# Loading the left half of B tile by tile instead of in pairs of tiles, in a matmul with RMS norm

## The chip, the cores and the metric

One core of a Trainium2 chip runs the whole program. The metric is the time of one execution on the device in microseconds (us). Runs of a kernel are compared with runs of the kernel before that were made on the same chip in the same rounds.

## The reference

```python
m, k, n = 2048, 2048, 2048          # a: m x k, b: k x n, float32
x = np.matmul(a, b)
rms = np.sqrt(np.mean(x ** 2, axis=-1, keepdims=True) + eps)
return (gamma * x / rms).astype(np.float32)
```

## The kernel before

Sixteen contraction tiles of 128 rows of B are handled as eight pairs. B is cut into a left and a right half of 1024 columns. In the head of the program the first four row blocks of A are multiplied with B while B is still arriving; later row blocks find all of B in the on-chip memory and use seven instead of eight products (Strassen's scheme) for each 2 x 2 of blocks. So only the head, about the first 57 us, can wait for B.

Left half: for each pair PE (TensorE) runs 7 matmuls with the first tile, 8 transposes for A of the next pair, 7 matmuls with the second tile, and 2 matmuls for the one block left over. (Pair 7, the last, has no next pair, and takes its matmuls block by block, so that its second matmul already needs the second tile.) The loads come from GpSimd's software queue and cast float32 to bfloat16 on the way: for each pair one load of A (four row blocks, 0.5 MB read), then one load of B (both tiles, 1 MB read).

```python
def load_b(j, kp):                       # j: half of B, kp: pair of contraction tiles
    nc.gpsimd.dma_start(
        out=raw[j][kp],                  # [128, 2, 1024] bf16
        in_=b[kp * W2:(kp + 1) * W2, j * HALF:(j + 1) * HALF].rearrange(
            "(t p) n -> p t n", p=P))

def load_head(kp):
    nc.gpsimd.dma_start(out=ah(kp), in_=a[0:HB * P, kp * W2:(kp + 1) * W2].rearrange(...))
    load_b(0, kp)
# ... pairs 1 to 3 are issued at the start; pair 0 comes over other queues ...
for kp in range(KP):                     # the left half
    if kp + 4 < KP:
        load_head(kp + 4)
    else:
        load_later(1)                    # right half of B, then A
    before = [lambda: transpose_head(kp + 1)] if kp + 1 < KP else []
    # ...
    stream(groups1, kp, before, ...)     # 7 matmuls, `before`, 7 matmuls
    # ...
    stream_in_parts(last1, kp)           # 2 matmuls
    # ... sums of B's quarters on DVE (VectorE) ...
# ...
for kp in range(KP):                     # the right half: 8 + 3 matmuls for a pair
    load_later(1)
    b_sums(1, kp)
    stream_right(kp)
    # ...
```

## Time and profile before

| | before |
|---|---|
| median of the first 3 runs | 222.82 us (222.45 to 223.1) |
| PE busy | 210.0 of 221.2 us |
| a left pair (A and B) lands every | 3.83 us; PE needs 3.89 us for it |
| a right pair of B lands every | 2.49 us; PE needs 2.38 us for it |

The page of the profile gives the span, the busy time of each engine, and the chain of work that ended last. PE is nearly always busy, and the loads of B are the only other large part of the chain. The profiled execution took 222.97 us, more than the median of this kernel's runs.

```profile
span 221.2 us, 3022 instructions
...
PE 210.0 (95%) x1035; PEld 97.7 (44%) x1035; DVE 167.4 (76%) x330; ACT 128.1 (58%) x263; POOL 29.4 (13%) x59
...
PE 83%; DMA 8%; POOL 3%; DVE 2%; issue 1%; ACT 1%; DVEq 0%; ACTq 0%; POOLq 0%
```

The timeline of PE in the head follows. The columns are start and duration in us, engine, source line, operation, output and inputs, and the count of merged instructions; brackets give idle time and what ended it. L384 are the head's matmuls, L172 the transposes, L415 the two extra matmuls, L289 the matmuls of the seven-product part.

```profile
12.30 1.67 PE L384 MATMUL acc<-b,head_at 128*128 128x512 bf16 x7
...
16.19 1.67 PE L384 MATMUL acc<-b,head_at 128*128 128x512 bf16 x7
...
20.18 1.67 PE L384 MATMUL acc<-b,head_at 128*128 128x512 bf16 x7
...
23.65 0.59 PE L415 MATMUL tbank<-b,head_at 128*128 128x512 bf16 x2
25.10 1.67 PE L384 MATMUL acc<-b,head_at 128*128 128x512 bf16 x7 [0.85 <-DMA b<-in_b_dram]
...
36.79 3.19 PE L384 MATMUL acc<-b,head_at 128*128 128x512 bf16 x14
...
54.28 1.89 PE L384 MATMUL acc<-b,head_at 128*128 128x512 bf16 x8
...
56.44 0.38 PE L289 MATMUL acc<-early,s 128*128 128x512 bf16 x1
56.69 0.59 PE L289 MATMUL acc<-b,s 128*128 128x512 bf16 x2
...
57.33 1.02 PE L384 MATMUL acc<-b,head_at 128*128 128x512 bf16 x4
```

Pairs 1 to 4 start at 12.30, 16.19, 20.18 and 25.10 us. Without waits they would be 3.89 us apart; pair 4 comes late, and the brackets show 0.85 us of it as a wait for B. The semaphores show what PE waits for. A load raises its semaphore once for each of 16 DMA engines, and these updates are in the trace. The Trainium skill ("DMA: Bandwidth & Descriptors", section "Why a DMA increments its semaphore by 16 and not by 1") says that only the full 16 means that all data has landed. Here are the times of the 8th and of the 16th update, read from the trace's semaphore records:

```
kernel before       8th engine   16th engine
B pair 3 (left)        19.83        20.38
A for pair 4           21.14        21.68
B pair 4 (left)        23.63        25.30
A for pair 5           24.96        26.69
B pair 5 (left)        27.47        29.11
B pair 6 (right)       52.49        54.45
B pair 7 (right)       55.02        56.88     (the last tile of B)
```

These times are counted from a zero about 0.24 us before the timeline's, as are all landings, packets and fetches below: on the timeline B pair 4 is complete at 25.05 us, and PE starts it at 25.10 us. With 0.24 us taken off, pairs 1, 3 and 4 start within 0.05 us of the moment when the *slowest* engine has delivered their tile. Pairs 2 and 5 to 7 follow the pair before without a gap, 0.1 to 0.3 us after their tile. One engine lags the middle one by 1.67 us from pair 4 on. In the right half PE gains nothing to spare either: it finishes the stage before pair 7 at 56.66 us (56.44 us plus one matmul step of 0.216 us) and starts the pair at 56.69 us, when the tile lands (56.64 us on the timeline).

### The profile page before, as it was taken

How to read it: one execution, taken by the hardware profiler on the slowest of the kernel's cores; microseconds unless marked ns; L12 is line 12 of the kernel's file. 1: busy time of each engine (PE TensorE's matmuls, PEld its weight loads, DVE VectorE, ACT ScalarE, POOL GpSimd, SP SyncE). 2: the span in 40 equal slices, each digit the busy share in tenths (PEclk: the TensorE clock that was granted, in tenths of full speed). 3: DMA queues.
4: the chain of work that ended last, by engine and by line, in shares of the span. 5: the costliest groups of instructions: out<-in, count | busy, mean ns of one | idle time of the engine just before them, and what ended most of it. 6: DMA issues, size and time to landing. Idle time of an engine off the chain costs nothing.

```text
span 221.2 us, 3022 instructions
## 1 busy us (share of the span) xinstructions
PE 210.0 (95%) x1035; PEld 97.7 (44%) x1035; DVE 167.4 (76%) x330; ACT 128.1 (58%) x263; POOL 29.4 (13%) x59
## 2 busy tenths in 40 slices
PE   7899899999999999999999999999999999999950
PEld 2445454444455444444444444444444444444430
DVE  2428789999988898969696639855794759797691
ACT  3110001830698898678945997389738995334570
POOL 7634323220000001200110002000200000000040
PEclk9999999999999999999999999999999999999996
DMA  6999999999938596956799249955798349044045
GB/s 184 223 202 209 203 208 210 211 211 238 426 114 357 187 291 120 316 230 150 219 308 397 79 88 266 367 221 95 187 302 367 69 90 381 32 190 193 1 190 191
DMA packets 36321, 47.13 MB, mean 213 GB/s; under 512 B 21969, under 2 KB 26065, under 8 KB 34897
## 3 DMA queue, kind: packets, MB, share of 16 engines
q0 software_dynamic: 9936, 23.33, 41.7%
q1 hardware_dynamic: 25936, 22.29, 33.6%
q10 hardware_dynamic: 432, 1.31, 2.0%
q8 instruction: 8, 0.13, 0.2%
q14 instruction: 9, 0.07, 0.1%
HBM read 34.60 MB, written 16.78 MB: 232 GB/s over the span
## 4 chain that ended last, share of the span: by engine, by line
PE 83%; DMA 8%; POOL 3%; DVE 2%; issue 1%; ACT 1%; DVEq 0%; ACTq 0%; POOLq 0%
PE acc L289 69%; PE acc L384 12%; DMA b<-in_b_dram 8%; POOL early L105 1%; POOL b L99 1%; DVE x L709 1%; PE tbank L415 1%; PE tbank L172 1%; DVE x L712 1%; ACT sq L307 0%; PE tbank L189 0%; PE acc L189 0%; DVE a L709 0%; ACT sq L778 0%; DVE x L786 0%
## 5 line engine op out<-in xcount | busy, mean ns | idle before, releaser
L289 PE MATMUL acc<-b,s 128*128 128x512 bf16 x408 | 92.1, 379 | 0.0
L289 PEld LDWEIGHTS <-s 128*128 128x128 f16 (+1 forms) x512 | 49.9, 98 | 59.9 <-DVE s L264 0.4
L384 PE MATMUL acc<-b,head_at 128*128 128x512 bf16 x176 | 41.9, 379 | 1.0 <-DMA b<-in_b_dram 0.9
L307 ACT ACTIVATE sq<-x 128x512 bf16<-128x512 f32 x54 | 34.0, 630 | 6.9 <-DVE x L709 3.0
L366 DVE SCALAR_TENSOR_TENSOR x<-x,r,gamma_sb 128x1024 f32<-128x1024 f32 x28 | 34.8, 1281 | 0.7
L223 ACT ACTIVATE sq<-a 128x1024 bf16<-128x1024 f32 x24 | 25.3, 1054 | 2.4 <-DMA a<-in_a_dram 1.9
L384 PEld LDWEIGHTS <-head_at 128*128 128x128 bf16 x176 | 16.8, 98 | 20.6 <-issue 1.9
L246 ACT ACTIVATE head_at<-a,s 128x2048 f16<-128x2048 f32 x10 | 20.0, 1998 | 3.7 <-DVE s L233 3.7
L426 ACT COPY x<-acc 128x512 f32<-128x512 f32 x6 | 3.4, 586 | 25.7 <-PE acc L384 25.7
L289 PEld LDWEIGHTS <-head_at 128*128 128x128 f16 (+1 forms) x112 | 10.9, 98 | 13.2
L289 PE MATMUL acc<-early,head_at 128*128 128x512 bf16 x64 | 14.5, 379 | 0.0
L289 PEld LDWEIGHTS <-at_even 128*128 128x128 f16 x96 | 9.4, 98 | 11.3
L289 PE MATMUL acc<-early,s 128*128 128x512 bf16 x56 | 14.4, 379 | 0.0
L264 DVE TENSOR_TENSOR s<-head_at 128x1024 f16<-128x1024 f16 (+5 forms) x22 | 13.4, 635 | 0.1
L596 DVE TENSOR_TENSOR x<-x,x 128x512 f32<-128x512 f32 x9 | 6.2, 692 | 8.8 <-ACT x L594 8.3
L99 POOL DMA_DIRECT2D b<-in_b_dram x15 | 10.6, 706 | 16.0 <-DMA b<-in_b_dram 13.4
L578 ACT COPY x<-acc 128x512 f32<-128x512 f32 x9 | 5.2, 574 | 11.6 <-PE acc L289 11.5
L289 PE MATMUL acc<-t_left,s 128*128 128x512 bf16 x48 | 11.3, 379 | 0.0
L280 DVE TENSOR_TENSOR b<-b 128x1024 bf16<-128x1024 bf16 x16 | 10.8, 684 | 0.2
L289 PE MATMUL acc<-t_left,head_at 128*128 128x512 bf16 x48 | 10.9, 379 | 0.0
L289 PE MATMUL acc<-t_left,at_even 128*128 128x512 bf16 x48 | 10.8, 379 | 0.0
L289 PE MATMUL acc<-early,at_even 128*128 128x512 bf16 x48 | 10.8, 379 | 0.0
(111 smaller groups left out, 216.7 us busy)
## 6 DMA issues: line engine op xcount, KB each, us to landing
out_dram<-x SPq DMA_DIRECT2D x30, 512.0 KB, 3.8
a<-in_a_dram POOLq DMA_DIRECT2D x10, 1024.0 KB, 8.7
b<-in_b_dram POOLq DMA_DIRECT2D x15, 512.0 KB, 17.5
a<-in_a_dram POOLq DMA_DIRECT2D x4, 512.0 KB, 16.6
early<-in_a_dram POOLq DMA_DIRECT2D x7, 256.0 KB, 14.8
early<-in_b_dram ACTq DMA_DIRECT2D x2, 512.0 KB, 5.9
gamma_sb<-in_gamma_dram POOLq DMA_DIRECT2D x1, 1024.0 KB, 14.8
early<-in_a_dram SPq DMA_DIRECT2D x1, 512.0 KB, 5.5
```

The costliest lines, as they stand in the source:

```text
L99: nc.gpsimd.dma_start(out=raw[j][kp], in_=b[kp * W2:(kp + 1) * W2, j * HALF:(j + 1) * HALF].rearrange("(t p) n -> p t n", p=P))
L223: nc.scalar.activation(out=junk, in_=a32[mb][:, h * HALF:(h + 1) * HALF], func=ACTF.Square, scale=2.0 ** -8, accum_out=n2[:, h:h + 1])
L246: nc.scalar.activation(out=a16[mb], in_=a32.pop(mb), func=ACTF.Copy, scale=factor.pop(mb))
L264: nc.vector.tensor_tensor(out=sum_of(g, s)[:, lo:hi, :], in0=x[:, lo:hi, :], in1=y[:, lo:hi, :], op=op)
L280: nc.vector.tensor_tensor(out=flat[:, 1:3, :], in0=flat[:, 1:3, :], in1=flat[:, 0::3, :], op=ALU.add)
L289: nc.tensor.matmul(bank, lhsT[:, kp, :], rhs, start=(start and kp == 0), stop=(kp == KP - 1), skip_group_check=not start)
L307: nc.scalar.activation(out=sq[:, 0:CH], in_=src, func=ACTF.Square, scale=inv_sqrt_n, accum_out=msq[mb][:, c:c + 1])
L366: nc.vector.scalar_tensor_tensor(out=x, in0=x, scalar=inverse_of[mb], in1=gamma_sb[:, h * HALF:(h + 1) * HALF], op0=ALU.mult, op1=ALU.mult)
L384: nc.tensor.matmul(bank, head_at[:, kt, r, :], head_rhs(c, kt), start=(kt == 0), stop=(kt == KT - 1))
L426: copy(out=x_chunk(*g), in_=banks[g])
L578: nc.scalar.copy(out=c, in_=one[1])
L596: nc.vector.tensor_tensor(out=t, in0=t, in1=x12, op=ALU.add)
```

## The change

In the left half each pair of B comes as two loads of one tile each. The intent is that PE can begin a pair when its first tile is there, without waiting for the second.

```diff
     def load_b(j, kp):
+        if j == 0:
+            for t in range(2):
+                lo = kp * W2 + t * P
+                nc.gpsimd.dma_start(out=raw[0][kp][:, t, :], in_=b[lo:lo + P, 0:HALF])
+            return
         nc.gpsimd.dma_start(
             out=raw[j][kp],
```

A comparison of the two built programs shows seven more loads on GpSimd and the same instructions in the same order on every other engine.

## The prediction

> What bounds the kernel now. PE is busy 210.0 of 221.2 us (table of busy time) and the chain that ended last is 83% PE, 8% the loads of B. PE starts each contraction pair of the head when its B tile has landed: in the timeline the first matmuls of pairs 1 to 4 start at 12.30, 16.19, 20.18 and 25.10 us, and the semaphore records of the trace complete for these tiles at 12.50, 16.33, 20.38 and 25.30. Only the last leaves a visible wait (0.85 us). Counting gaps against a full pair (3.89 us of PE work), PE loses about 1.3 us there. From pair 5 PE is as fast as the loads.
>
> The loads are one saturated stream until 62 us: a pair of the head (0.5 MB of A, 1 MB of B read) lands every 3.83 us, a right-half pair of B every 2.49 us, about 410 to 420 GB/s read, while PE needs 2.38 us for a right-half pair. So PE, which enters the right half with about 0.8 us in hand, loses it: at 54.28 and 56.69 us it starts pairs 6 and 7 within some 0.03 us of their landing (54.45 and 56.88 in the records, which run 0.2 us behind PE). From there to 208 us PE has no idle gap. The end of the kernel is tied to the landing of the last right-half tile, not to PE's progress in the left half.
>
> What the change does. Seven loads of 1 MB become fourteen of 0.5 MB; bytes, casts, order of the queue and every other engine's order stay the same (the comparison of instruction order shows nothing else).
> - The first tile of each pair lands about 1.25 us earlier, the second when the pair did. This removes most of the 0.85 us wait at pair 4 and the small ones: up to 1.3 us, all in the left half.
> - GpSimd issues more: 0.70 us for a pair now, against 2 x 0.55 us estimated from the half-block loads (0.53 to 0.57). 1.9 us of issue for each 3.83 us of transfer: not limiting.
> - A software load is issued only when the one eight places before it has landed (the waits of GpSimd). Eight in flight now mean 15 us of transfer, afterwards about 10 us: still deep enough to keep the stream full.
> - Each extra load adds its completion. The half-size loads of A land every 1.25 us, 0.015 us more than half a 2.49 us pair: 7 x 0.015 = 0.1 us later for everything behind (estimate). The Trainium skill, "DMA: Bandwidth & Descriptors", section "Bandwidth", advises batches of at least 1 MiB; this trace shows next to no loss at 0.5 MB in a full queue.
>
> On the critical path. The gain dies in the right half, since b's last tile still lands at about 56.9 us; the 0.1 us of delay stays. The Trainium skill, same page, section "Why a DMA increments its semaphore by 16 and not by 1", says that all 16 engines must finish: here one engine lags the others by 1.3 us after an instruction fetch at 21.7 us, which makes the 25.1 us stall; that lag persists.
>
> Prediction: 222.9 us, 222.3 to 223.5; faster by over 2%: 1%, within 2%: 97%, slower: 2%.
>
> What would show it: no wait of PE at 25 us; PE ahead by about 1 us at 37 us; new waits of PE on B between 44 and 57 us adding up to the same; pair 7 of the right half again at 56.7 to 56.9 us; unchanged timeline after.
>
> What would make it wrong: the stream running dry with fewer bytes in flight (slower by 1 us or more), or the last tile landing earlier because the lag of the one engine shrinks (faster by up to 1 us).

## The result, and the profile after

| | before | after |
|---|---|---|
| median of 6 runs | 222.53 us (222.14 to 223.1) | 222.88 us (222.63 to 223.7) |
| ratio | | 1.0021, 95% interval 0.9998 to 1.0045 |
| profiled run: span | 221.2 us | 221.1 us |

A ratio is the mean time of one kernel's runs over that of the other's runs of the same rounds; it is not quite the ratio of the medians quoted beside it. The small difference points to slower, and it came again when the kernel was timed a second time (1.0019, 1.0003 to 1.0036).

The page and the timeline of PE of the changed kernel follow (lines are numbered five higher: L389 the head's matmuls, L177 the transposes, L420 the extra matmuls, L294 the seven-product part). Some records of matmuls are missing from this trace (1015 of 1035).

```profile
span 221.1 us, 3016 instructions
...
PE 209.8 (95%) x1015; PEld 97.9 (44%) x1035; DVE 167.0 (76%) x330; ACT 128.0 (58%) x263; POOL 31.9 (14%) x66
...
PE 89%; DVE 4%; DMA 3%; issue 1%; ACT 1%; DVEq 0%; ACTq 0%
```

```profile
12.43 1.46 PE L389 MATMUL acc<-b,head_at 128*128 128x512 bf16 x6
...
16.33 1.67 PE L389 MATMUL acc<-b,head_at 128*128 128x512 bf16 x7
18.30 0.62 PE L177 MATMUL tbank<-identity,early 128*128 128x128 bf16 x8 [0.30 <-DVE t_left L280]
...
20.70 1.67 PE L389 MATMUL acc<-b,head_at 128*128 128x512 bf16 x7
...
24.60 1.67 PE L389 MATMUL acc<-b,head_at 128*128 128x512 bf16 x7
26.11 0.61 PE L177 MATMUL tbank<-identity,early 128*128 128x128 bf16 x8
...
36.30 3.19 PE L389 MATMUL acc<-b,head_at 128*128 128x512 bf16 x14
...
54.08 1.89 PE L389 MATMUL acc<-b,head_at 128*128 128x512 bf16 x8
...
56.24 0.38 PE L294 MATMUL acc<-early,s 128*128 128x512 bf16 x1
56.61 0.59 PE L294 MATMUL acc<-b,s 128*128 128x512 bf16 x2
...
57.25 1.02 PE L389 MATMUL acc<-b,head_at 128*128 128x512 bf16 x4
```

The 0.85 us wait at the start of pair 4 is gone: pair 4 starts at 24.60 instead of 25.10 us. The share of DMA in the chain falls from 8% (loads of B) to 3%, and these 3% are the very first load of A, before which nothing can start. PE is 0.49 us ahead at pair 7 (36.30 against 36.79 us). It is 0.20 us ahead at right pair 6 (54.08 against 54.28), and 0.08 us at right pair 7 (56.61 against 56.69). The table of landings shows the right half's gate in the old place:

```
changed kernel          8th engine   16th engine
A for pair 3               17.29        18.50
B pair 4, tile 1           22.38        23.62
B pair 4, tile 2           23.64        24.83
A for pair 5               25.00        26.17
B pair 7 (right)           55.08        56.81     (the last tile of B)
```

Against this trace, then, the left half saves 0.49 us, less than predicted, and the right half takes it back. Most of the 0.49 us comes from the long lag of one engine in this trace of the kernel before: in the second trace of that kernel (shown below) left pair 7 starts at 36.36 us, so that the lead is 0.06 us. What replaced the wait for B is seen in the list of waits, of PE's weight loads (PEld) from 8 to 58 us. The columns are engine, line, what it waited for, then us in total, times, longest. First before, then after:

```profile
PEld L172 <- DMA early<-in_a_dram: 0.2, 1, 0.2
```

```profile
PEld L177 <- DMA early<-in_a_dram: 1.2, 3, 0.8
```

The transposes, which stand halfway through a pair, now wait for A of the next pair: 1.2 us in three waits, against 0.2 us in one. These are idle times of the weight loads. PE itself lost about 0.46 us, once, at 18.30 us: the bracket there names DVE, but the weight load beside it waits for A, and A for pair 3 was complete only at 18.50 us (18.26 us on the timeline). Its slowest engine was 1.21 us behind the middle one. From there to pair 7 PE has no gap.

GpSimd was no limit. Its issues show in the DMA table (size written, median us from issue to landing), before and after. Only eight software loads are in flight at a time (before the change the ninth is issued at 10.00 us, after the first has landed at 9.72 us, both on the timeline), so the smaller loads also wait a shorter time in the queue:

```profile
b<-in_b_dram POOLq DMA_DIRECT2D x15, 512.0 KB, 17.5
...
early<-in_a_dram POOLq DMA_DIRECT2D x7, 256.0 KB, 14.8
```

```profile
b<-in_b_dram POOLq DMA_DIRECT2D x8, 512.0 KB, 16.0
b<-in_b_dram POOLq DMA_DIRECT2D x14, 256.0 KB, 10.0
...
early<-in_a_dram POOLq DMA_DIRECT2D x7, 256.0 KB, 10.0
```

### The profile page after: what moved, and what is told of

The parts are those of the page before. It is cut to its first block, busy times and chain, and to the rows that moved or that the text cites. A ratio compares the mean times of both kernels' runs of the same rounds, so it can differ in the third digit from the quotient of the medians.

```text
span 221.1 us, 3016 instructions
## 1 busy us (share of the span) xinstructions
PE 209.8 (95%) x1015; PEld 97.9 (44%) x1035; DVE 167.0 (76%) x330; ACT 128.0 (58%) x263; POOL 31.9 (14%) x66
## 4 chain that ended last, share of the span: by engine, by line
PE 89%; DVE 4%; DMA 3%; issue 1%; ACT 1%; DVEq 0%; ACTq 0%
PE acc L294 69%; PE acc L389 16%; DMA early<-in_a_dram 3%; PE tbank L420 2%; PE tbank L177 2%; DVE x L714 1%; DVE x L717 1%; DVE t_left L280 0%; ACT sq L312 0%; PE tbank L194 0%; PE tbank L160 0%; PE acc L194 0%; DVE head_at L182 0%; DVE x L426 0%; DVE a L714 0%
## 5 line engine op out<-in xcount | busy, mean ns | idle before, releaser
L294 PE MATMUL acc<-b,s 128*128 128x512 bf16 x397 | 91.5, 379 | 0.6
L294 PEld LDWEIGHTS <-s 128*128 128x128 f16 (+1 forms) x512 | 49.9, 98 | 60.0 <-DVE s L269 0.4
L389 PE MATMUL acc<-b,head_at 128*128 128x512 bf16 x171 | 41.3, 379 | 0.3
L389 PEld LDWEIGHTS <-head_at 128*128 128x128 bf16 x176 | 16.8, 98 | 19.5 <-issue 0.7
L431 ACT COPY x<-acc 128x512 f32<-128x512 f32 x6 | 3.4, 587 | 24.8 <-PE acc L389 24.8
L294 PEld LDWEIGHTS <-head_at 128*128 128x128 f16 (+1 forms) x112 | 11.0, 98 | 13.2
L294 PE MATMUL acc<-early,head_at 128*128 128x512 bf16 x63 | 14.4, 379 | 0.1
L294 PEld LDWEIGHTS <-at_even 128*128 128x128 f16 x96 | 9.4, 98 | 11.3
L294 PE MATMUL acc<-early,s 128*128 128x512 bf16 x55 | 14.2, 379 | 0.0
L294 PE MATMUL acc<-t_left,s 128*128 128x512 bf16 x47 | 11.3, 379 | 0.1
L131 POOL COPY pace<-x 128x1 f32<-128x1 f32 x4 | 1.7, 413 | 66.3 <-DVE x L610 65.1
L294 PE MATMUL acc<-early,at_even 128*128 128x512 bf16 x48 | 10.8, 379 | 0.1
L294 PE MATMUL acc<-t_left,head_at 128*128 128x512 bf16 x48 | 10.9, 379 | 0.0
L294 PE MATMUL acc<-t_left,at_even 128*128 128x512 bf16 x47 | 10.8, 379 | 0.1
```

The lines of the kernel that those rows point to most:

```text
L294: nc.tensor.matmul(bank, lhsT[:, kp, :], rhs, start=(start and kp == 0), stop=(kp == KP - 1), skip_group_check=not start)
L389: nc.tensor.matmul(bank, head_at[:, kt, r, :], head_rhs(c, kt), start=(kt == 0), stop=(kt == KT - 1))
```

## The experiments

The following theories were tested. **G (gate):** what the left half gains, the right half gives back, because its tiles land when they did before. **A (next wait):** within the left half, the load of A for the next pair, behind both tiles, is the next thing PE meets, so splitting B alone gains little. **C (cost) and S (slow packets):** the extra loads themselves cost time, by their completions, or because single packets become slow. **F (fetch)**: the wait at pair 4 comes from a fetch of PE's own instructions. A packet of a B load takes 173 ns (median); packets over 300 ns are called slow below, and their counts are read from the trace's DMA records.

### The changed kernel again

> The changed kernel once more, for a second trace. Theory G (gate): PE gains in the left half and gives it back in the right half, because each right-half tile lands when it did before; the first matmuls of right pair 7 start at 56.6 to 56.8 us as before, ratio 1.000 (0.998 to 1.002). Rival C (cost): the extra loads delay the whole stream and eat the gain; then the last right-half tile lands at least 0.3 us later than the 56.88 us of before. If the two slow packets at 14.6 us of the first trace are chance, they are absent here, and PE is ahead by 0.9 us instead of 0.5 us at left pair 7 (35.9 instead of 36.3 us).

Measured: median 223.09 us (222.51 to 223.39) against 222.48 us, ratio 1.0019 (1.0003 to 1.0036). The profiled run was one of the fast ones (222.57 us).

```profile
PEld L177 <- DMA early<-in_a_dram: 2.4, 6, 0.9
```

```profile
24.03 1.67 PE L389 MATMUL acc<-b,head_at 128*128 128x512 bf16 x7
26.11 0.62 PE L177 MATMUL tbank<-identity,early 128*128 128x128 bf16 x8 [0.41 <-DMA early<-in_a_dram]
26.57 1.67 PE L389 MATMUL acc<-b,head_at 128*128 128x512 bf16 x7
...
36.31 3.19 PE L389 MATMUL acc<-b,head_at 128*128 128x512 bf16 x14
```

What follows: the last right-half tile landed at 56.49 us, and right pair 7 started at 56.29 us, earlier than the forecast 56.6 to 56.8 us. The sign that was named for C, a landing 0.3 us or more after 56.88 us, is absent. But C is not out: 56.88 us is of a slow trace, and the middle engine landed this tile at 55.24 us, 0.22 us later than before (55.02 us). The wait for A is there again, 2.4 us in six waits of the weight loads, one of them right after pair 4's first matmuls (26.11 us, where PE itself stood 0.41 us). The slow packets came again: before 35 us this trace has seven, the first trace of the change two (1148 and 1058 ns at 14.6 us). What they take above 173 ns each sums to 2.0 and 1.9 us. Four traces of kernels with pair loads (`before` twice, `short_pair`, `warm44_pair`) have one, two, one and four, with sums of 0.2 to 0.6 us. Left pair 7 started at 36.31 us again, not at the 35.9 us that I had expected in their absence.

### The right half's stream shortened, with pairs and with split loads

The edit fills half of the first right-half tile instead of loading it; everything behind it lands 1.25 us earlier. `short_pair` is the kernel before with it, `short_split` the changed kernel. Their outputs are wrong, which doesn't matter for the times.

```diff
     def load_b(j, kp):
+        if (j, kp) == (1, 0):
+            nc.gpsimd.dma_start(out=raw[1][0][:, 0, :], in_=b[0:P, HALF:N])
+            nc.gpsimd.memset(raw[1][0][:, 1, :], 0.5)
+            return
```

> Wrong result on purpose: half of the first right-half tile is filled by GpSimd instead of loaded, so 0.5 MB less is read and everything behind it lands 1.25 us earlier; left loads as in the kernel before. Theory G: PE was only just tied to the stream here (0.03 us), so it gains next to nothing: right pair 7 starts at 56.6 to 56.7 us (before 56.69), ratio 0.999 to 1.001. Rival C makes the same forecast here; it differs in the next run.

> The same shortened stream with the left loads split. Theory G: with the gate moved 1.25 us earlier, PE keeps what it gained in the left half: right pair 7 starts 0.4 to 1.0 us before that of short_pair, the span is shorter than that of short_pair by as much unless the row chain behind the A blocks catches it, ratio to before 0.996 to 0.998. Rival C: no lead to keep, pair 7 within 0.2 us of short_pair and ratio 0.999 to 1.001.

Measured: `short_pair` 222.40 us (222.27 to 222.45), ratio 0.9993 (0.9980 to 1.0006), as expected; but its trace starts right pair 7 at 55.98 us, not at the forecast 56.6 to 56.7 us, which suggests that the traced execution of the kernel before had lost more to the gate than a usual one. `short_split`: the profiled execution took 580.91 us, with PE at about a third of its usual rate. It is used for nothing; its granted clock was 1.00, so why it was slow stays open. The five others are 222.36, 222.43, 222.60, 223.80 and 223.89 us, ratio 1.0020 (0.9994 to 1.0047).

What follows: my forecast for `short_split` (0.996 to 0.998) failed. With the right half's gate moved out of the way the plain split still does not win, and its runs scatter over 1.5 us where those of the pair form lie within 0.2 us. So G is not the whole story: the plain split loses something in the left half already, in some executions and not in others.

### Work that does not need the newest tile

`fill_split` is the changed kernel with five matmuls of the seventh product moved forward into right pairs 5 to 7, to give PE something to do while a tile is late.

```diff
+        if kp == 5:
+            pair[7] = ps_t.tile([P, CH], FP32, name="tbank")
+        for k in {5: (0, 1, 2), 6: (3,)}.get(kp, ()):
+            product_matmul(PAIR, 1, 7, pair[7], k)      # and k = 4 at pair 7
...
-    product(PAIR, 1, 7, p7, within={5: [lambda: turn(HB, 0)]})
-    turn(HB, 1)
+    product_matmul(PAIR, 1, 7, p7, 5)
+    product_matmul(PAIR, 1, 7, p7, 6)
+    turn(HB, 0)
+    product_matmul(PAIR, 1, 7, p7, 7)                  # turn(HB, 1) after 2 of product 6
```

> Right result. The changed kernel with five matmuls of the seventh product moved from behind the right half into its last three pairs, so that PE has work there that does not wait for the newest tile. Theory G: PE keeps the 0.3 us of lead that it has at right pair 5 and ends 0.2 to 0.4 us earlier than the changed kernel, ratio to before 0.998 to 0.9995. Rival C: no gain, ratio 1.000 or above. If the row chain (square sums, factor, scaling) now holds the turn of the first A block, the gain is lost there and PE shows a wait at about 63.5 us.

Measured: 223.16 us (222.9 to 223.89), ratio 1.0032 (1.0017 to 1.0048). It is slower, by 0.3%. The trace shows the wait that the expectation named as the way to lose, at the first turn of a new A block (L194):

```profile
64.07 0.59 PE L294 MATMUL tbank<-b,s 128*128 128x512 bf16 x2
65.19 0.62 PE L194 MATMUL acc<-identity_h,head_at 128*128 128x128 f16 x8 [0.52 <-ACT sq L228]
```

The last right-half tile landed at 57.34 us in this trace, with nine slow packets before 35 us. The row chain (square sums on ACT, ScalarE, then factor and scaling on DVE) starts when the last right-half products are done, so it is late with that tile, and PE, which had used up its other work earlier, waited for it. A gain at one gate would meet this next one.

### A between the two tiles

By the landings of the changed kernel, half a pair takes 1.25 us of the stream and A 1.34 us. After the start s of a pair, PE needs A for the next pair at s + 1.51 us and the second tile at s + 1.96 us (7 matmul steps of 0.216 us, then transposes of 0.45 us). If the first tile lands at L, the plain split delivers the second tile at L + 1.25 and A at L + 2.59, so s cannot be before L + 1.08. With the pair load s is L + 1.25. The split alone is therefore worth 0.17 us against the stream. With A between the two tiles s is L + 0.63, a gain of 0.62 us. `inter_split` has this order; `inter_short` has it and the shortened right half.

```diff
-        nc.gpsimd.dma_start(out=ah(kp), ...)  # A
-        load_b(0, kp)                         # tile 1, tile 2
+        if kp == 1:
+            load_a(1)
+        half_b(0)
+        if kp + 1 < KP:
+            load_a(kp + 1)
+        half_b(1)
```

> Right result. Split left loads, but the A tile of the next pair is loaded between the two tiles of a pair. Theory A (A gate): in the changed kernel PE is held at the transposes by the next pair's A tile, which still comes behind both B tiles; from the landings (1.25 us for half a pair, 1.34 us for A) and PE's needs (A 1.51 us after the start of a pair, second B tile 1.96 us) the split alone lets PE start a pair 0.17 us earlier against the stream, this order 0.62 us. So the waits of the transposes for A (1.2 and 2.4 us summed in the two traces of the changed kernel) go below 0.5 us and left pair 7 starts 0.3 to 0.5 us earlier than with the plain split for the same lag of the slowest engine. The right half gives it back: ratio to before 0.999 to 1.003, not below the kernel before. Rival: the A waits stay, the loss being random slow packets alone.

> Wrong result on purpose: the same order with 0.5 MB of the right half filled instead of loaded, so that no landing gates the right half. Theory A with slow packets: median 222.0 to 222.5 us, spread over the runs below 0.8 us (the shortened plain split had 222.36 to 223.89, the shortened pair form 222.27 to 222.45). If slow packets in the left half alone decide it: spread again over 1 us, median above 222.7.

Measured: `inter_split` 222.82 us (222.58 to 223.09) against 222.41 us, ratio 1.0013 (1.0000 to 1.0027). `inter_short` 222.08 us (222.02 to 222.27), ratio 0.9980 (0.9968 to 0.9992). The waits of `inter_split` (L400 the head's matmuls, L431 the extra matmuls; the transposes' line, L188, has none):

```profile
PE acc L400 <- DMA b<-in_b_dram: 0.5, 2, 0.3
PE tbank L431 <- DVE head_at L193: 0.4, 1, 0.4
```

```profile
26.14 1.67 PE L400 MATMUL acc<-b,head_at 128*128 128x512 bf16 x7 [0.26 <-DMA b<-in_b_dram]
...
35.88 3.40 PE L400 MATMUL acc<-b,head_at 128*128 128x512 bf16 x14
...
44.08 1.89 PE L400 MATMUL acc<-b,head_at 128*128 128x512 bf16 x8
...
46.86 1.89 PE L400 MATMUL acc<-b,head_at 128*128 128x512 bf16 x8 [0.24 <-DMA b<-in_b_dram]
...
56.35 0.59 PE L305 MATMUL acc<-b,s 128*128 128x512 bf16 x2
...
57.00 1.24 PE L400 MATMUL acc<-b,head_at 128*128 128x512 bf16 x5
```

```profile
span 220.3 us, 3035 instructions
```

```profile
35.72 3.38 PE L404 MATMUL acc<-b,head_at 128*128 128x512 bf16 x14
...
56.41 1.89 PE L404 MATMUL acc<-b,head_at 128*128 128x512 bf16 x8
```

What follows. Theory A holds: with A between the tiles the transposes no longer wait for A, and left pair 7 starts at 35.88 us, 0.42 us earlier than with the plain split. About 0.2 us of this is lost at once: pair 7 takes 3.40 instead of 3.19 us, because its second matmul waits for the second tile. Theory G holds too: in `inter_split` PE stops in the right half (46.86 us, a bracketed wait for B; that tile's 16th engine came at 47.06 us), and no time is saved. The gate in this trace is that tile, right pair 3, and not the last one: its slowest engine was 1.89 us behind the middle one, against 1.25 us for the next tile, just after an instruction fetch at 45.03 us. From there PE runs without a gap to right pair 7 (56.35 us; its tile was complete at 56.20 us on the timeline). Where the right half is shortened, PE has no wait on the stream after pair 1 but the 0.2 us inside left pair 7, every run is faster than the median before, and the ratio is below 1 with its whole interval. Another thing was not forecast: neither trace has a single slow packet before 35 us. `inter_short` does not scatter either. In its edit it differs from `short_split` only in the place of A's load, so the order of the loads is the likely cause of the scatter; with five runs of each, timed in different rounds on different chips, this is not proven.

### The number of loads, and their size

`tiny_short` keeps the pair loads, shortens the right half, and adds an 8 KB software load after each left pair. `four` is the changed kernel with each tile of the left half in two loads of 64 partitions.

```diff
# tiny_short
         load_b(0, kp)
+        nc.gpsimd.dma_start(out=x_slot[6][0:16, kp * P:(kp + 1) * P],
+                            in_=b[kp * W2:kp * W2 + 16, 0:P])
# four
-                nc.gpsimd.dma_start(out=raw[0][kp][:, t, :], in_=b[lo:lo + P, 0:HALF])
+                for p in range(0, P, 64):
+                    nc.gpsimd.dma_start(out=raw[0][kp][p:p + 64, t, :],
+                                        in_=b[lo + p:lo + p + 64, 0:HALF])
```

> Wrong result on purpose: left loads by pairs as in the kernel before, right half shortened, and after each left pair one extra software load of 8 KB into space not used yet. Number of loads, issue times and depth of the queue are then those of the split, the B loads those of before. Theory S (slow packets come with more software loads in a shallower queue): packets of over 0.3 us in two engines between 14 and 31 us, together over 1 us per engine, and runs spread over 222.3 to 223.8 us. Rival (they come with the smaller B loads themselves): as the shortened pair form, 222.3 to 222.7 us, slow packets under 0.7 us per engine.

> Right result. Each left pair in four loads of 0.25 MB (64 partitions of a tile each), 21 loads more than before, so eight in flight are about 6 us of transfer. Theory G with completions at 0.01 us each: the middle engine lands the last right-half tile 0.2 us later than before (55.0 to 55.3 us), ratio 1.000 to 1.004. Theory S: more slow packets than in the split, last landing 0.5 to 1.5 us later than the middle engine's, ratio 1.003 to 1.008. If the depth of the queue matters by itself, the middle engine falls behind by over 0.5 us too.

Measured: `tiny_short` 222.46 us (222.44 to 222.82), ratio 1.0000 (0.9987 to 1.0012), no slow packet before 35 us. `four` 223.34 us (222.61 to 224.78), ratio 1.0042 (1.0016 to 1.0068), 17 slow packets before 35 us and 34 more from there to 56 us. In `four` the middle engine landed the last right-half tile at 56.83 us, 1.8 us later than before (55.02 us), and the 16th at 57.67 us.

What follows: S as forecast here (slow packets come with more loads in a shallower queue) is not supported. In this trace as many software loads and as shallow a queue as in the split make no slow packets, when the B loads stay whole. `tiny_short` is also the control for `inter_short`, in the same rounds: with pair loads (and the 8 KB loads) the moved gate gave 1.0000, not 0.9980. The rival fits the traces: slow packets come with B pieces loaded back to back, and more of them with smaller pieces. In `four` the whole stream fell behind as well, much more than 21 completions of 0.01 us; smaller pieces and a queue of about 6 us changed together there, so which of the two did it stays open.

### Whose delay makes the wait at pair 4

`warm44_pair` is the kernel before with the same warm-up time for PE in four times as many, smaller matmuls, so that PE's instruction stream is 33 matmuls with their weight loads longer.

```diff
-    for _ in range(11):
-        nc.tensor.matmul(warm_bank, warm[:, 0:P], warm[:, 0:CH], start=True, stop=True)
+    for _ in range(44):
+        nc.tensor.matmul(warm_bank[:, 0:P], warm[:, 0:P], warm[:, 0:P], start=True, stop=True)
```

> Right result. The kernel before, with 44 warm-up matmuls of 128 columns in place of 11 of 512: the same PE time, but 33 matmuls with their weight loads more in PE's instruction stream. Theory F (the lag that makes the wait at pair 4 is PE's own instruction fetch, 16 KB on one engine for 0.97 us at 21.7 us): the fetch comes about 33 matmuls, 5 to 6 us, earlier, at 15.5 to 17.5 us, one engine lags by 0.7 to 1.3 us from the tile that lands next (pair 2 or 3), and the visible wait moves from the start of pair 4 to that pair. Rival (the lag belongs to a place in the load stream): it stays at pair 4. Ratio 0.998 to 1.003 either way.

Measured: 222.73 us (222.54 to 223.53), ratio 1.0015 (0.9995 to 1.0035). The first 16 KB transfer of the instruction queue came at 17.56 us instead of 21.72 us, and the wait moved to pair 3:

```profile
18.25 1.67 PE L384 MATMUL acc<-b,head_at 128*128 128x512 bf16 x7
...
20.79 1.67 PE L384 MATMUL acc<-b,head_at 128*128 128x512 bf16 x7 [0.44 <-DMA b<-in_b_dram]
...
22.74 1.67 PE L384 MATMUL acc<-b,head_at 128*128 128x512 bf16 x7
...
24.68 1.67 PE L384 MATMUL acc<-b,head_at 128*128 128x512 bf16 x7
```

What follows: F holds, on one trace. Pair 4 (24.68 us) follows without a wait. The wait that the change was to remove is made by a fetch of PE's own instructions, which takes 0.94 to 0.98 us of one engine's time, and the tile is complete only when that engine has done its share. The trace does not number the engines, so that it is the same engine is argued from the times.

### The kernel before again

> The kernel before as it is, for a second trace, since the first one (222.97 us) is at the slow end of its runs (222.3 to 223.3). If the 0.85 us wait at left pair 4 is typical, it shows again; if the first trace had an unusually large lag of one engine, the wait is 0.2 to 0.5 us here, the last right-half tile lands at 56.2 to 56.6 us instead of 56.88, and the span is near 220.7 us. Ratio 1.000 (0.998 to 1.002).

Measured: 222.47 us (222.32 to 223.14), ratio 0.9997 (0.9980 to 1.0014). The profiled run is the slowest of the four (223.14 us), span 221.4 us. In it the wait at pair 4 is 0.42 us, and there is a wait at right pair 7:

```profile
24.66 1.67 PE L384 MATMUL acc<-b,head_at 128*128 128x512 bf16 x7 [0.42 <-DMA b<-in_b_dram]
...
36.36 3.18 PE L384 MATMUL acc<-b,head_at 128*128 128x512 bf16 x14
...
56.85 0.59 PE L289 MATMUL acc<-b,s 128*128 128x512 bf16 x2 [0.36 <-DMA b<-in_b_dram]
```

What follows: the last right-half tile landed at 57.05 us, and the span is 0.2 us longer than in the first trace although PE was 0.43 us *ahead* of it at left pair 7 (36.36 against 36.79 us). Progress in the left half does not decide the time; the landing of the last tile does. Seven traces with the whole right half in its old order (`before` and `after` twice each, `warm44_pair`, `inter_split`, `four`) bear this out: the last landing ranges from 56.36 to 57.67 us, and the span is 164.3 to 164.4 us longer than it in each. (In `warm44_pair` and `inter_split` PE reached that tile 0.1 us or a little more after its landing, so there it did not wait.) The size of the wait at pair 4 varies from run to run (0.85 and 0.42 us here, 0.33 us in `short_pair`, 0.16 us in `tiny_short`), so the 1.3 us read from the first trace was more than a usual run has to offer. The forecast that this trace would be a faster one failed.

### Both halves split, with A between

`inter_both` is `inter_split` with the right half's tiles split too, and with the last right pair's matmuls reordered so that those of the first tile come first.

```diff
-        if j == 0:
+        if True:                     # both halves by tiles
...
-            for m in (2, 5):
-                pair_matmul(m, kp)
+            pair_matmul(2, kp)
             pair_matmul(1, kp - 1)
+            order = [(g, 2 * kp) for g in plain] + [(g, 2 * kp + 1) for g in plain]
-        for g, kt in order:
+        for n, (g, kt) in enumerate(order):
+            if kp == KP - 1 and n == 6:
+                pair_matmul(5, kp)
```

> Right result. Left half as in the interleaved order; the right half's tiles are split too, and the last right pair runs the first tile's matmuls before those that need the second. Theory G: each right pair can start up to 1.25 us earlier against the same landings, so the lead survives to the end of the right half (last right pair starts 0.3 to 0.6 us earlier than in inter_split) unless the row chain holds the turn of the first A block at 63.8 us; ratio to before 0.998 to 1.000. If halves of a tile loaded back to back bring slow packets again, as in the plain split, packets of over 0.3 us appear between 37 and 57 us, and the ratio is 1.001 to 1.004.

Measured: 222.57 us (222.4 to 223.42) against 222.59 us, ratio 1.0001 (0.9985 to 1.0016). What follows: it undoes the loss but wins nothing. The wait of the first A block's turn for the row chain grew from 0.4 to 0.6 us, so part of the lead met that next gate, as in `fill_split`. Slow packets came again where halves of tiles followed each other (three of 412 to 741 ns at 36 us). No version with a right result beat the kernel before.

## Why the prediction was right or wrong

- **The time** was right: 222.88 us (and 223.09 us in the repeat) lies in 222.3 to 223.5. That 222.88 us is so close to the forecast 222.9 us is luck: the forecast started from 222.82 us, the median of three runs, where six gave 222.53 us, and the measured loss of 0.35 us is larger than the 0.1 us it added. The gain was to die in the right half. Between the first two traces it did: PE's lead was 0.49 us at left pair 7 and 0.08 us at right pair 7, where the tile's 16th engine came at 56.81 us against 56.88 us. Against the second trace of the kernel before there was hardly a gain to lose (0.06 us). That a landing in the right half is the gate is shown by `inter_split` against `inter_short`: the same left half gives nothing with the gate in place and 0.2% when it is moved, while with pair loads moving it gives nothing clear of noise (0.9993 in `short_pair`, 1.0000 in `tiny_short`).
- **No wait of PE at the start of pair 4**: right; it was 0.85 us and is gone.
- **"Up to 1.3 us, all in the left half"**, with PE ahead "by about 1 us at 37 us": too large; it was 0.49 us against the first trace of the kernel before and 0.06 us against the second. The failed step is "The first tile of each pair lands about 1.25 us earlier, the second when the pair did. This removes most of the 0.85 us wait". It counted what B allows and left out A for the next pair, which comes behind both tiles and is needed halfway through a pair. That next wait leaves 0.17 us of a lead against the stream; `inter_split` removed it. The rest of the 0.49 us I put down to the different lag of the slowest engine in the two traces; the wait itself is 0.16 to 0.44 us in the four other traces with pair loads.
- **"New waits of PE on B between 44 and 57 us"**: partly. No wait carries that label in the first trace after, since each gap is 0.15 us or less; they show in the starts of the pairs, and with the label in `inter_split`.
- **"7 x 0.015 = 0.1 us later for everything behind (estimate)"**: about right for the middle engine, which landed the last tile at 55.08 and 55.24 us in the two traces of the change and at 55.29 us in `fill_split`, 0.06 to 0.27 us after 55.02 us. (The half-size loads of A follow each other by 1.27 us in the trace of the kernel before, not by 1.25 us.) The step that was too small is that nothing but completions was charged to the split. Its cost was about 0.2% (1.0021 and 1.0019), some 0.4 us. Part of it can be this delay of the middle engine. It also comes with slow packets in the left half: 1.9 and 2.0 us of excess before 35 us in the two traces of the change, 0.2 to 0.6 us in four traces with pair loads. Against it stand `inter_short` and `tiny_short`, with none and with a tight spread. That slow packets *cause* the 0.4 us is argued from this; neither trace of the change is of one of its slower executions (223.2 to 223.7 us).
- **"That lag persists"**, from an instruction fetch: right; the slowest engine is 1.67 us behind the middle one at pair 4 and 1.86 us at the last tile. The fetch as cause is shown by `warm44_pair`, on one trace.
- **What stays open**: why packets of a half-size load become slow when it directly follows the other half, and not when A's load is between. Traces in which only that order differs show the packets in one and not in the other; the mechanism is not shown. How much of the 0.4 us is slow packets and how much the later middle engine is open too.

## What to carry to other kernels

Before a load is cut to start a consumer sooner, list everything that the consumer needs next from the same saturated queue, in order: the gain ends at the second item. Here it was 0.17 us by that count, and not the 1.25 us by which the first item moved. Then look for the last transfer that gates the same engine further on; if it does not move, neither does the end. And loads that take as long in total can still differ in their slowest packets, so compare the spread of the runs and the last engine's landing as well as the rate.

## What the Trainium skill lacked or had wrong

- "Runtime: NRT & Kernel Launch", section "Instruction fetch mechanics", says that instructions are refilled in blocks of 16 KiB (256 instructions), and that the cost of crossing such a boundary is "mostly hidden". The trace agrees with the size: eight transfers of 16,384 bytes on the instruction queue. But the page lacks that a fetch can delay an engine that carries data: it took 0.975 us at 21.7 us, and PE waited for B for 0.85, 0.42 and 0.44 us in three traces, in the third at the earlier place to which the fetch had moved. That both use the same engine is inferred from the times.
- "DMA: Bandwidth & Descriptors", section "Bandwidth", advises batches of 1 MiB or more. In a full queue it made little difference to the rate here: 0.5 MB of B every 1.25 us, 1 MB every 2.49 us. What small loads cost is another thing, which no page has: slow packets. When the two tiles of a pair were loaded one directly after the other, two to nine packets took 301 to 1148 ns instead of 173 ns before 35 us (three traces: the change twice and `fill_split`); in three traces with another load between them none did before 35 us.
- The same page, section "Latency and other measured facts", says that DMA engines 7 and 15 are usually slower, with a guess at the cause. Here most slow packets of the split come as two at a time (1148 and 1058 ns at 14.6 us, 546 and 525 ns at 26.2 us), which would fit two engines; but the trace does not number the engines, so no run here shows which they are.
